# A hybrid encoder's up projections: four chunks by seven products in place of six, begun one tile ahead, with their block sums on VectorE

## The chip, the cores and the metric

The kernel runs on one core of one Trainium2 chip. The metric is the device time of one execution in microseconds (us); of several runs the median is given. A second number per kernel comes from a profiled execution, whose trace has the start and the end of every instruction on TensorE (PE; its weight loads apart as PEld), VectorE (DVE), ScalarE (ACT), GpSimd (POOL) and the DMA queues.

## The reference

Two layers, one sequence of 512 tokens, 1024 features, all in float32. Layer 1 mixes the tokens by gated linear attention, layer 2 by grouped-query softmax attention. Each mixer is followed by the gated feed-forward part (FFN) that this change is about:

```python
D_MODEL, SEQ, DEPTH, D_FF = 1024, 512, 2, 2816

def conv_ffn(h, w_up, w_conv, b_conv, w_down):
    u = h @ w_up                                  # 1024 -> 2 x 2816
    u = lax.conv_general_dilated(u, w_conv[:, None, :], window_strides=(1,),
        padding=[(1, 1)], dimension_numbers=('NWC', 'WIO', 'NWC'),
        feature_group_count=u.shape[-1]) + b_conv # each feature: 3 tokens
    val, gate = jnp.split(u, 2, axis=-1)
    return (jax.nn.silu(gate) * val) @ w_down     # 2816 -> 1024

x = x + mixer(rmsnorm(x, norm_mix[i]))
x = x + conv_ffn(rmsnorm(x, norm_ffn[i]), ...)
```

## The kernel before

**Tiles.** Activations lie with features on the 128 partitions and the 512 tokens in the free dimension: `x` is eight tiles of 128x512 (`KC` = 8). The 2 x 2816 up features are 22 chunks `m` (`FC` = 22). A chunk has two tiles of 128 features, the value tile (t = 0) and the gate tile (t = 1).

**Precision.** A float32 product is made from three products of a rounded type (`F32R`): every operand is split into a high part (a ScalarE copy) and a low part (a VectorE subtraction), and the kernel adds high x high, high x low and low x high. A plain tile is thus 8 blocks of features x 3 = 24 matmuls of 512 columns, and a plain chunk 48. These are the matmuls of lines 359 to 361.

**Seven products.** A pair of tiles times pairs of input blocks is a 2x2 block product. It can be made by seven products of blocks in place of eight, from sums and differences of the blocks. The down projection does this for chunks 0 to 15, in two parts (`down_part`, four strips of weights each, `NQ` = 4), and so do the up projections of the chunks in `SEVEN`: 7 products of 12 matmuls of 256 columns, 84 in all (line 810, in `product`). The accumulators are the `r` banks of PSUM. What a chunk by seven products needs beside a plain one:

- sums of the four weight blocks (`Weights.summed`, lines 158, 159, 166 and 172; the argument `by` says on which engine, GpSimd for up and VectorE for down), then the splits of four pieces. Piece 0 serves the products 1 and 7, piece 1 the products 6 and 5, piece 2 the products 2 and 4, and piece 3 product 3 (`PLACE`). Piece 2 gets its low part by an accumulating DMA that GpSimd issues (`flush`, line 194).
- differences of the input blocks, made once per layer for the four pairs of feature blocks (`prepare_input(p)`, called after chunk p = 0 to 3; tiles `x1`, `x2`, `q`, `xt`). The two subtractions of 256 columns there (lines 889, 890) run on GpSimd, and so do those of `prepare` (lines 866, 867), which does the same for the FFN's middle activations (`gu`) ahead of the down projection.
- sums of products. `seven_up` avoids some by copying a bank into another and letting the next product accumulate on the copy: product 1 is copied into the second bank (line 820), the sum of 1 and 6 into the third (`r3`, the copy below it). Product 3 accumulates on the second bank after its contents were copied to the output tile `d` (line 829). At the end come VectorE's additions and the multiplication by the norm's factor `R`.

After either kind of chunk `act_up` does the convolution: one ScalarE step (line 848) and two VectorE steps of 511 columns (849, 850) per tile, then the activation (852) and the product of the two tiles (853).

**Weights ahead.** `Weights.todo` is the list of all weight pieces in the order in which they are made. A piece is a strip's load into one of two `raw` tiles, perhaps its sums, and its split into `wh` and `wl` (three buffers each, line 204 on ScalarE and 205 on VectorE; `ring`, one buffer, for piece 1 of the sums; `sq`, three buffers, for piece 3). `W.piece(..., ahead)` hands out a piece and makes so many more that `ahead` stand ready; the table `ahead` in `ffn` raises that number near a chunk or part by seven products.

**Order.** The loop at the end of `ffn` runs over m: `act_up(m)`, for m < 4 `prepare_input(m)`, after every second chunk `prepare` or the plain splits, and after m = 9 and m = 17 a part of the down projection (`DOWN_AFTER`). That part is a generator: its product 1 and the copy after it are issued inside `plain_up(m)`, between the chunk's two tiles, and the rest after the chunk. The chunks 16 to 21 go down by plain matmuls at the end, in the order of `PLAIN`. Each engine runs its own instructions in the order in which they are issued here, and waits for others by semaphores. PSUM has three banks `acc` (value tiles, the first two product banks), two `s` (gate tiles, the third bank), two `pt` and one `po`.

## Time and profile before

| | |
|---|---|
| median of three runs | 1145.89 us (1145.68 to 1147.14) |
| profiled execution | 1147.76 us, of which the span from the first to the last instruction is 1146.0 |
| mean granted TensorE clock | 0.990 |
| read from HBM | 100.21 MB |

How to read the rows below. A row of the page names an engine, its busy time in us, the share of the span and the number of instructions. In the stretches (windows), the columns are start:end in us from the span's start, length, then busy us (instructions) of PE, PEld, DVE, ACT and POOL, the mean granted clock (1.00 is full speed), the busy share of the DMA engines, and GB/s. A row of the timeline has start, duration, engine, line, operation, output<-inputs, sizes, and in brackets what the instruction waited for and how long. A row of the waits says which instruction waited for which, total us, times, longest. Lines are those of the kernel before.

### The profile page before, as it was taken

Reading aid. Unit: us, or ns where it says so; the run is one execution under the profiler, and the core shown is the slowest. Engines: PE = TensorE matmul, PEld = TensorE weight load, DVE = VectorE, ACT = ScalarE, POOL = GpSimd, SP = SyncE. Lnnn points to the kernel's source line nnn. Section 1 sums busy time; section 2 is a strip of 40 time slices with the busy share of each in tenths; the row PEclk is TensorE's granted clock in tenths of the full one; section 3 lists DMA queues with packets and bytes.
Section 4 is the critical chain, followed back from the end, with each engine's and each line's share of the span. In section 5 each row is a group of like instructions: output and inputs, shape, how many; then the busy total and the mean of one; then the engine's idle time right before and its main releaser. Section 6 shows DMA issues by size and latency. Waiting matters only on the chain.

```text
span 1146.0 us, 16132 instructions
## 1 busy us (share of the span) xinstructions
PE 1110.6 (97%) x6212; PEld 967.6 (84%) x6212; DVE 863.5 (75%) x1333; ACT 630.2 (55%) x1022; POOL 210.0 (18%) x202
## 2 busy tenths in 40 slices
PE   9999999997999999999999999999799999999998
PEld 7888888885889988899888888788588998889887
DVE  6686774679988778887765588567998877988772
ACT  5565343546656456665464777555664645656550
POOL 0100122014311131122004333001431112112300
PEclk9999999998999999999999999999899999999999
DMA  6323122322416433354447755432241544335442
GB/s 223 132 90 110 56 92 74 111 74 59 129 71 165 134 125 106 103 145 134 144 144 166 193 166 156 129 110 74 58 130 71 159 136 129 95 96 151 139 129 74
DMA packets 33149, 136.91 MB, mean 119 GB/s; under 512 B 4016, under 2 KB 4528, under 8 KB 22704
## 3 DMA queue, kind: packets, MB, share of 16 engines
q1 hardware_dynamic: 21072, 102.16, 25.9%
q0 software_dynamic: 7104, 25.17, 11.2%
q10 hardware_dynamic: 4896, 8.55, 2.0%
q8 instruction: 49, 0.80, 0.3%
q14 instruction: 28, 0.23, 0.1%
HBM read 100.21 MB, written 2.10 MB: 89 GB/s over the span
## 4 chain that ended last, share of the span: by engine, by line
PE 75%; DVE 11%; issue 5%; ACT 4%; POOL 3%; DMA 2%; ACTq 0%; POOLq 0%; DVEq 0%; SPq 0%
PE r L810 17%; PE vg L391 8%; PE op L417 8%; PE up L359 7%; PE up L360 7%; PE up L361 7%; PE dn L360 2%; PE dn L361 2%; PE dn L359 2%; DVE wl L205 1%; DVE y L849 1%; DVE gu L860 1%; DVE y L853 1%; DVE u L798 1%; PE o L685 1%
## 5 line engine op out<-in xcount | busy, mean ns | idle before, releaser
L359 PE MATMUL up<-xhl,wh 128*128 128x512 f32 x512 | 200.7, 392 | 7.3 <-ACT wh L204 7.3
L361 PE MATMUL up<-xhl,wl 128*128 128x512 f32 x512 | 199.5, 390 | 0.6 <-DVE wl L205 0.6
L360 PE MATMUL up<-xhl,wh 128*128 128x512 f32 x512 | 199.9, 391 | 0.0
L204 ACT ACTIVATE wh<-raw 128x1024 fp32r<-128x1024 f32 x108 | 114.0, 1056 | 146.1 <-PE up L360 51.7
L205 DVE TENSOR_TENSOR wl<-raw,wh 128x1024 fp32r<-128x1024 f32 x108 | 131.8, 1220 | 44.2 <-ACT wh L204 43.7
L359 PEld LDWEIGHTS up<-xhl,wh 128*128 128x128 f32 x512 | 96.4, 188 | 27.1 <-ACT wh L204 7.8
L810 PE MATMUL r<-gu,wh 128*128 128x256 f32 x640 | 116.7, 283 | 0.1
L361 PEld LDWEIGHTS up<-xhl,wl 128*128 128x128 f32 x512 | 96.2, 188 | 21.3 <-DVE wl L205 1.4
L360 PEld LDWEIGHTS up<-xhl,wh 128*128 128x128 f32 x512 | 96.5, 188 | 19.0
L810 PEld LDWEIGHTS r<-gu,wh 128*128 128x128 f32 x640 | 99.6, 191 | 0.8 <-ACT r L934 0.5
L194 POOL DMA_DIRECT2D wl<-raw x44 | 39.2, 890 | 287.1 <-ACT wl L145 76.3
L810 PE MATMUL r<-gu,wl 128*128 128x256 f32 x320 | 90.5, 283 | 1.0 <-DMA wl<-raw 1.0
L848 ACT ACTIVATE y<-u,cw 128x512 f32<-128x512 f32 x88 | 69.9, 810 | 35.9 <-DVE u L798 25.4
L391 PE MATMUL vg<-wh,xhl 128*128 128x512 f32 x256 | 80.9, 395 | 1.0 <-DVE wh L202 1.0
L417 PE MATMUL op<-oT,wh 128*128 128x512 f32 x256 | 71.8, 394 | 0.6 <-ACT p L1137 0.6
L849 DVE SCALAR_TENSOR_TENSOR y<-u,cw,y 128x511 f32<-128x511 f32 x88 | 66.3, 766 | 6.7 <-ACT y L848 6.7
L850 DVE SCALAR_TENSOR_TENSOR y<-u,cw,y 128x511 f32<-128x511 f32 x88 | 67.2, 780 | 1.2
L810 PEld LDWEIGHTS r<-gu,wl 128*128 128x128 f32 x320 | 61.1, 191 | 1.2 <-DMA wl<-raw 1.2
L810 PE MATMUL r<-xhl,wh 128*128 128x256 f32 x288 | 56.5, 294 | 4.1 <-ACT u L829 3.7
L391 PEld LDWEIGHTS vg<-wh,xhl 128*128 128x128 f32 x256 | 48.9, 191 | 11.5 <-ACT sq L333 1.3
L798 DVE TENSOR_TENSOR u<-up,R 128x512 f32<-128x512 f32 x64 | 43.5, 683 | 17.5 <-PE up L361 17.5
L859 ACT ACTIVATE gu<-y 128x512 fp32r<-128x512 f32 (+1 forms) x60 | 33.9, 572 | 41.2 <-POOL y L867 19.3
(266 smaller groups left out, 2591.4 us busy)
## 6 DMA issues: line engine op xcount, KB each, us to landing
raw<-in_w_up_dram SPq DMA_DIRECT2D x42, 1024.0 KB, 4.9
wl<-raw POOLq DMA_DIRECT2D x44, 512.0 KB, 4.6
raw<-in_w_down_dram SPq DMA_DIRECT2D x22, 1024.0 KB, 4.9
raw<-in_w_vg_dram SPq DMA_DIRECT2D x6, 1024.0 KB, 4.9
ring<-p ACTq DMA_DIRECT2D x22, 256.0 KB, 3.4
raw<-in_w_kq_dram SPq DMA_DIRECT2D x4, 1024.0 KB, 4.8
raw<-in_w_gout_dram SPq DMA_DIRECT2D x4, 1024.0 KB, 5.0
raw<-in_w_aout_dram SPq DMA_DIRECT2D x16, 256.0 KB, 4.8
```

Source lines behind the costliest of these rows:

```text
L204: act.activation(hi[:, sl], r[:, sl], AF.Copy)
L205: dve.tensor_tensor(lo[:, sl], r[:, sl], hi[:, sl].bitcast(F32), ALU.subtract)
L359: mm(ps, wh, mh, start=start, stop=False)
L360: mm(ps, wh, ml, start=False, stop=False)
L361: return mm(ps, wl, mh, start=False, stop=stop)
L391: mm(ps[j][:, :width], hl[k][i == 2][:, j * P : (j + 1) * P], (wl if i == 1 else wh)[:, sl], start=k == 0 and i == 0, stop=k == KC - 1 and ...
L417: mm(pss[ng][n], wt[:, sl], mv, start=k == 0 and i == 0, stop=k == KC - 1 and i == 2)
L798: dve.tensor_tensor(u, ps, norm.R, ALU.mult)
L810: mm(dst, w[:, sl], m, start=start and j == 0 and a == 0, stop=j == len(pairs) - 1 and a == 2, skip_group_check=True)
L848: act.activation(y, u, AF.Identity, scale=w(1), bias=w(3))
L849: dve.scalar_tensor_tensor(y[:, 1:], u[:, : S - 1], w(0), y[:, 1:], ALU.mult, ALU.add)
L850: dve.scalar_tensor_tensor(y[:, : S - 1], u[:, 1:], w(2), y[:, : S - 1], ALU.mult, ALU.add)
```

## The change

The chunks by seven products become 5, 12, 19 and 21 in place of 4, 6, 12, 14, 18 and 20. They are begun as the parts of the down projection are: `seven_up` is now a generator that `plain_up` of the chunk before starts after its first tile, and that stops after product 1 and the copy into the second bank. `add_up` moves the first piece of its weights ahead of the second half of the chunk before, and the table `ahead` gets the same three entries as for a down part. Products 7 and 6 change places. Product 3 gets a bank `r5` of its own; its output half is then a copy of that bank and an addition from the second bank, and the fourth bank is copied to both halves of `d`, to which the second and third banks are added. That makes five copies of 256 columns on ScalarE per chunk where there were four. All block sums and differences that GpSimd did go to VectorE.

```diff
-SEVEN = (4, 6, 12, 14, 18, 20)
+SEVEN = (5, 12, 19, 21)
...
-        def summed(self, raw, h, by):
+        def summed(self, raw, h):
             a21, a11, a12, a22 = (raw[:, n * S : (n + 1) * S] for n in range(4))
             if h == 0:
                 r = tmp("t", "sum")
                 with tc.issue_after(self.last.ins) if self.last else ExitStack():
-                    by.tensor_tensor(r, a21, a11, ALU.add)
-                    by.tensor_tensor(a21, a21, a22, ALU.add)
+                    dve.tensor_tensor(r, a21, a11, ALU.add)
+                    dve.tensor_tensor(a21, a21, a22, ALU.add)
...
             if h == 1:
-                by.tensor_tensor(a11, a21, a11, ALU.add)
+                dve.tensor_tensor(a11, a21, a11, ALU.add)
...
-                by.tensor_tensor(r, a11, a12, ALU.add)
+                dve.tensor_tensor(r, a11, a12, ALU.add)
...
     def add_up(layer, chunks):
         for m in chunks:
-            W.add(up[layer], (m,), 4 if m in SEVEN else 2, pool)
+            W.add(up[layer], (m,), 4 if m in SEVEN else 2)
+            if m in SEVEN:
+                W.todo[-5:-3] = W.todo[-4], W.todo[-5]
...
         ahead = {(m + i // 2, i % 2): n for m in DOWN_AFTER for i, n in ((-1, 2), (0, 2), (1, 5))}
-        ahead.update({(m - 1, t): 2 for m in SEVEN for t in range(2)})
+        ahead.update({(m - 1 + i // 2, i % 2): n for m in SEVEN for i, n in ((-1, 2), (0, 2), (1, 5))})
...
                 feature_tile(*W.half(up[layer], 2 * m + t, ahead.get((m, t), 1)), norm.hl, ps)
                 pss.append(ps)
+                if t == 0 and m + 1 in SEVEN:
+                    begun.append(seven_up(m + 1))
+                    next(begun[-1])
...
-            r1, r2 = (bank("acc", n)[:, :H] for n in ("r1", "r2"))
+            r1 = bank("acc", "r1")[:, :H]
             go(1, r1, True)
+            r2 = bank("acc", "r2")[:, :H]
             act.activation(r2, r1, AF.Copy)
-            r4 = bank("pt", "r4")[:, :H]
-            go(7, r4, True)
+            yield
             go(6, r2, False)
             r3 = bank("s", "r3")[:, :H]
             act.activation(r3, r2, AF.Copy)
+            r4 = bank("pt", "r4")[:, :H]
+            go(7, r4, True)
             go(2, r1, False)
+            c, d = tmp("u", "u"), tmp("u", "u")
+            dve.tensor_tensor(c[:, :H], r1, norm.R[:, :H], ALU.mult)
             go(5, r2, False)
-            c, d = tmp("u", "u"), tmp("u", "u")
-            act.activation(d[:, H:], r2, AF.Copy)
-            dve.tensor_tensor(c[:, :H], r1, norm.R[:, :H], ALU.mult)
             go(4, r3, False)
-            dve.tensor_tensor(d[:, H:], d[:, H:], r4, ALU.add)
-            go(3, r2, False)
-            act.activation(d[:, :H], r3, AF.Copy)
-            dve.tensor_tensor(d[:, :H], d[:, :H], r4, ALU.add)
-            dve.tensor_tensor(c[:, H:], r2, norm.R[:, H:], ALU.mult)
+            r5 = bank("pt", "r5")[:, :H]
+            go(3, r5, True)
+            act.activation(d[:, :H], r4, AF.Copy)
+            act.activation(d[:, H:], r4, AF.Copy)
+            dve.tensor_tensor(d[:, H:], d[:, H:], r2, ALU.add)
+            dve.tensor_tensor(d[:, :H], d[:, :H], r3, ALU.add)
+            act.activation(c[:, H:], r5, AF.Copy)
+            dve.tensor_tensor(c[:, H:], c[:, H:], r2, ALU.add)
+            dve.tensor_tensor(c[:, H:], c[:, H:], norm.R[:, H:], ALU.mult)
             yield c
...
-            for t, u in enumerate((seven_up if m in SEVEN else plain_up)(m)):
+            for t, u in enumerate(begun.pop() if m in SEVEN else plain_up(m)):
...
-            pool.tensor_tensor(q[:, :H], b22, b12, ALU.subtract)
-            pool.tensor_tensor(b12, b11, b12, ALU.subtract)
+            dve.tensor_tensor(q[:, :H], b22, b12, ALU.subtract)
+            dve.tensor_tensor(b12, b11, b12, ALU.subtract)
```

The last four lines stand for `prepare` and `prepare_input` alike.

What this does to the order of the instructions is seen at two places. The first is ScalarE's queue around chunk 12 of the first layer, which is by seven products before and after. `r` are the product banks, `y` the convolution's tiles, `raw` a strip of weights, `wh` the high part of its split; `wh_3734` and `wh_3752` before, `wh_3609` and `wh_3613` after are the two halves of the plain chunk 13's weights. Before:

```order
L848 ACTIVATE y_3665<-u_3663,cw 128x512
L204 ACTIVATE wh_3734<-raw_3732 128x1024
L848 ACTIVATE y_3671<-u_3669,cw 128x512
L820 ACTIVATE r_3694<-r_3693 128x256
L204 ACTIVATE wh_3752<-raw_3732 128x1024
L852 ACTIVATE y_3671<-y_3671 128x512
L825 ACTIVATE r_3750<-r_3694 128x256
```

After:

```order
L827 ACTIVATE r_3598<-r_3576 128x256
L859 ACTIVATE y_3643<-u_3641,cw 128x512
L204 ACTIVATE wh_3609<-raw_3607 128x1024
L859 ACTIVATE y_3649<-u_3647,cw 128x512
L831 ACTIVATE r_3683<-r_3598 128x256
L204 ACTIVATE wh_3613<-raw_3607 128x1024
L863 ACTIVATE y_3649<-y_3649 128x512
```

The copy into the second bank (L820, now L827) stood behind a weight split and two convolution steps and now stands ahead of them. The copy into the third bank (L825, now L831) stood behind both splits of chunk 13 and now stands between them.

The second place is VectorE's queue in the second layer, where the `ring` tile of the layer's first chunk by seven products (m = 4 before, m = 5 after) gets its low part on line 188. `xt` are the split input differences, `gu` those of the middle activations, `q` differences, `sum` a sum of weight blocks. Before:

```order
L205 TENSOR_TENSOR wl_7585<-raw_7522,wh_7584 128x1024
L849 SCALAR_TENSOR_TENSOR y_7560<-u_7558,cw,y_7560 128x511
L163 TENSOR_TENSOR wl_7594<-raw_7588,wh_7593 128x512
L850 SCALAR_TENSOR_TENSOR y_7560<-u_7558,cw,y_7560 128x511
L893 SCALAR_TENSOR_TENSOR q_7568<-x_7566,x_7567 128x256
L163 TENSOR_TENSOR wl_7594<-sum_7590,wh_7593 128x512
L853 TENSOR_TENSOR y_7554<-y_7554,y_7560 128x512
L860 TENSOR_TENSOR xt_7573<-x_7566,xt_7573 128x256
L860 TENSOR_TENSOR xt_7574<-q_7568,xt_7574 128x512
L895 SCALAR_TENSOR_TENSOR x_7567<-q_7568,x_7567 128x256
L188 TENSOR_TENSOR ring_7625<-raw_7588,ring_7625 128x1024
L860 TENSOR_TENSOR xt_7573<-x_7567,xt_7573 128x256
```

After:

```order
L871 TENSOR_TENSOR xt_7565<-x_7558,xt_7565 128x256
L906 SCALAR_TENSOR_TENSOR x_7559<-q_7560,x_7559 128x256
L871 TENSOR_TENSOR xt_7566<-q_7560,xt_7566 128x512
L878 TENSOR_TENSOR y_7444<-y_7444 128x256
L871 TENSOR_TENSOR xt_7565<-x_7559,xt_7565 128x256
L871 TENSOR_TENSOR gu_7579<-y_7546,gu_7579 128x512
L871 TENSOR_TENSOR gu_7578<-y_7444,gu_7578 128x512
L885 SCALAR_TENSOR_TENSOR q_7575<-y_7444,y_7546 128x256
L188 TENSOR_TENSOR ring_7622<-raw_7509,ring_7622 128x1024
L887 SCALAR_TENSOR_TENSOR y_7546<-q_7575,y_7546 128x256
```

Before, the `ring` tile's low part came among the last inputs of pair 3, ahead of the split of `x_7567`. Now it comes after all inputs, and after two of the splits of the middle activations (`gu`) of the chunks 2 and 3, with the subtraction of line 878, which was GpSimd's, in the same queue.

More of the change, by code (lines that the diff above doesn't have):

```diff
@@ L120, in __init__, with add @@
             self.todo, self.made, self.raw, self.by_dma, self.pending = [], {}, {}, [], []
-            self.sums, self.last, self.fine = {}, None, []
-        def add(self, src, strips=None, pieces=2, by=None):
+            self.sums, self.last, self.fine = set(), None, []
+        def add(self, src, strips=None, pieces=2):
             for i in strips or range(src.shape[0]):
@@ L126, in add @@
                 if pieces > 2:
-                    self.sums[id(src), i] = by
+                    self.sums.add((id(src), i))
         def make(self, key):
@@ L138, in make @@
             if (id(src), i) in self.sums:
-                self.made[id(src), i, h] = self.summed(self.raw[id(src), i], h, self.sums[id(src), i])
+                self.made[id(src), i, h] = self.summed(self.raw[id(src), i], h)
                 return
@@ L234, in add_ffn @@
             add_up(layer, range(first, m + 1))
-            W.add(down_w[layer], range(part * NQ, (part + 1) * NQ), 4, dve)
+            W.add(down_w[layer], range(part * NQ, (part + 1) * NQ), 4)
             at = len(W.todo) - 4 * NQ - 1
@@ L780, in ffn @@
         inputs = []
+        begun = []
         def plain_up(m):
@@ L888, in prepare_input @@
             b11, b12, b21, b22 = y1[:, :H], y1[:, H:], y2[:, :H], y2[:, H:]
-            pool.tensor_tensor(q[:, :H], b22, b12, ALU.subtract)
-            pool.tensor_tensor(b12, b11, b12, ALU.subtract)
+            dve.tensor_tensor(q[:, :H], b22, b12, ALU.subtract)
+            dve.tensor_tensor(b12, b11, b12, ALU.subtract)
             t = [big(F32R, "xt") for _ in range(2)]
```

## Prediction

> **What bounds the kernel now.** I read the page first, then busy time by stretch of the two feed-forward (FFN) layers, with the stretches cut at the first matmul of each chunk in TensorE's timeline, then TensorE's waits, and last the rows of the engines that it waits for. The page's first part says that TensorE (PE) is the bound:
>
> ```profile
> PE 1110.6 (97%) x6212; PEld 967.6 (84%) x6212; DVE 863.5 (75%) x1333; ACT 630.2 (55%) x1022; POOL 210.0 (18%) x202
> ```
>
> So a gain has to be TensorE work that goes, or a wait of TensorE that goes. The stretches tell what a chunk costs there (columns: length in us, busy us and instructions of PE, PEld, DVE, ACT, POOL, then the granted clock, DMA share, GB/s). First layer:
>
> ```profile
> 273.11:318.79 45.68, 35.76 (x218) 31.71 (x216) 42.04 (x58) 28.54 (x46) 16.72 (x15) 0.89 0.39 116
> 391.61:413.39 21.78, 21.78 (x98) 18.03 (x97) 14.47 (x18) 8.85 (x13) 6.38 (x5) 1.00 0.23 78
> 413.39:425.53 12.14, 10.28 (x86) 10.06 (x84) 8.58 (x12) 6.42 (x11) 3.92 (x4) 1.00 0.63 206
> 436.44:447.83 11.39, 10.54 (x85) 10.13 (x84) 9.75 (x15) 6.89 (x13) 1.82 (x2) 1.00 0.72 220
> 475.06:520.96 45.90, 45.85 (x361) 44.67 (x360) 38.75 (x61) 29.05 (x44) 9.83 (x9) 1.00 0.62 168
> 520.96:530.99 10.03, 10.03 (x87) 10.03 (x85) 4.74 (x8) 4.68 (x8) 2.26 (x2) 1.00 0.63 220
> 541.89:552.22 10.33, 10.29 (x85) 10.08 (x84) 7.63 (x11) 5.94 (x10) 0.89 (x1) 1.00 0.69 210
> ```
>
> 391.61 to 413.39 is two plain chunks (m = 10, 11): 10.89 us each, no wait. 520.96 to 530.99 is a chunk by seven products (m = 18) without a wait: 84 matmuls of 256 columns in 10.03 us, 0.119 us each. Seven products are worth only 0.86 us a chunk, so a wait of one microsecond eats the gain. And they wait: m = 12 takes 12.14 us, m = 14 11.39, m = 20 10.33. The first row holds the chunks 4, 5 and 6; without the plain chunk 5 it is 45.68 - 10.89 = 34.79 us for two, 14.73 more than 2 x 10.03. The second layer is alike:
>
> ```profile
> 817.62:864.40 46.78, 36.75 (x217) 32.42 (x216) 42.98 (x61) 29.53 (x47) 16.67 (x15) 0.85 0.38 113
> 959.01:971.11 12.10, 10.26 (x85) 10.06 (x84) 8.56 (x12) 6.52 (x11) 3.92 (x4) 1.00 0.66 207
> 982.02:993.42 11.40, 10.55 (x85) 10.14 (x84) 9.76 (x15) 6.91 (x13) 1.82 (x2) 1.00 0.77 229
> 1067.78:1077.81 10.03, 10.03 (x87) 10.03 (x86) 4.91 (x8) 4.44 (x9) 2.58 (x2) 1.00 0.70 228
> 1088.71:1098.73 10.02, 10.02 (x85) 10.01 (x84) 7.09 (x11) 5.71 (x9) 0.39 (x1) 1.00 0.77 231
> ```
>
> The twelve chunks cost 34.79 + 12.14 + 11.39 + 10.03 + 10.33 = 78.68 and 35.89 + 12.10 + 11.40 + 10.03 + 10.02 = 79.44, together 158.1 us: more than twelve plain ones (130.7). TensorE's waits in the second layer (total us, times, longest) say for whom:
>
> ```profile
> PE r L810 <- ACT r L820: 4.2, 3, 1.8
> PE up L359 <- ACT wh L204: 3.6, 1, 3.6
> PE r L810 <- ACT u L829: 1.8, 1, 1.8
> PE r L810 <- DVE xt L860: 1.8, 1, 1.8
> PE r L810 <- DMA wl<-raw: 1.0, 1, 1.0
> ```
>
> L820 copies product 1 into the second bank, behind which only product 7 (12 matmuls, 1.43 us) runs before the copy is needed. L829 copies the bank away before product 3 overwrites it. L204 and L860 are weights and inputs of the layer's first such chunk, which begins before they are made. The last is an accumulating DMA, issued by GpSimd behind its sums; after the change GpSimd's queue holds only such DMAs in the FFN, and as this wait came once in sixteen strips I count nothing for it.
>
> **The change, part by part.** *Fewer such chunks.* Eight remain and four become plain. Without any wait this is 8 x 10.03 + 4 x 10.89 = 123.8 us against 158.1, a saving of 34.3 less the waits R that the new form still has.
>
> *Begun one tile ahead.* Product 1 now stands ahead of the second tile of the plain chunk before, so its copy has 5.44 us (a tile) of cover, not 1.43, and the L820 waits go. The down projection already begins so: its 336 matmuls and one plain tile fill 475.06 to 520.96, and (45.90 - 5.44) / 4 = 10.11 us per 84 matmuls leaves no wait.
>
> *Third product in its own bank.* Product 3 waits for no copy, so the L829 waits go. ScalarE makes five copies of 256 columns per chunk in place of four, 0.36 us beside matmuls: nothing.
>
> *Product 7 after product 6.* This holds the first weight tile longer, and there is the new wait. How a ScalarE queue stalls TensorE is seen in chunk 6 before, first on ScalarE, then on TensorE:
>
> ```profile
> 309.99 0.81 ACT L848 ACTIVATE y<-u,cw 128x512 f32<-128x512 f32 x1 [1.49 <-DVE u L798]
> 310.71 0.36 ACT L820 ACTIVATE r<-r 128x256 f32<-128x256 f32 x1
> 311.01 1.04 ACT L204 ACTIVATE wh<-raw 128x1024 fp32r<-128x1024 f32 x1
> ```
>
> ```profile
> 311.13 1.71 PE L810 MATMUL r<-xt,ring 128*128 128x256 f32 x12 [1.84 <-ACT r L820]
> ```
>
> The copy sat behind an instruction that waited. In the new order the copy into the third bank sits behind the weight split of the next chunk, and that split waits until product 7 has freed its buffer. From then ScalarE does the split (1.04), in chunks 12 and 21 a convolution step (0.72 to the next start), and the copy (0.36): 2.12 us. The cover is product 2, 1.43 us; product 5, which overwrites the copied bank, comes next. That leaves 0.7, and 0.2 for the hand-overs (the copy ends at 311.07, TensorE starts at 311.13; a matmul of 256 columns runs 0.28 us for a 0.12 us slot): 0.9 us in chunks 12 and 21, 0.2 in chunk 19, where the convolution step is not in between. In chunk 5 it is more: two copies of inputs stand there in the first layer, 0.57 each by
>
> ```profile
> L859 ACT ACTIVATE gu<-y 128x512 fp32r<-128x512 f32 (+1 forms) x60 | 33.9, 572 | 41.2 <-POOL y L867 19.3 <-DVE y L853 11.5 <-DVE y L876 10.3
> ```
>
> so 1.04 + 1.14 + 0.36 - 1.43 + 0.2 = 1.3. In the second layer two splits, one such copy and one of half the size (0.36) give 2 x 1.04 + 0.57 + 0.36 + 0.36 - 1.43 + 0.2 = 2.1. First layer 1.3 + 0.9 + 0.2 + 0.9 = 3.3, second 2.1 + 2.0 = 4.1. The bounds: nothing, if the split is early as in the down projection, and 2.1 each, what chunk 12 loses now.
>
> *The sums on VectorE.* It takes 16 sums of 512 columns (4 chunks x 4) and 24 subtractions of 256 (12 pairs x 2) per layer from GpSimd. One would fear for an engine that was busy 42.04 of 45.68 us in the first stretch. But look at what GpSimd did to it there, GpSimd first:
>
> ```profile
> 272.15 1.28 POOL L159 TENSOR_TENSOR raw<-raw 128x512 f32<-128x512 f32 x1
> 274.95 1.62 POOL L172 TENSOR_TENSOR sum<-raw 128x512 f32<-128x512 f32 x1
> ```
>
> ```profile
> 272.22 1.50 DVE L893 SCALAR_TENSOR_TENSOR q<-x,x 128x256 f32<-128x256 f32 x1 [1.87 <-POOL x L890]
> 273.64 1.78 DVE L163 TENSOR_TENSOR wl<-sum,wh 128x512 fp32r<-128x512 f32 x1
> 275.35 1.77 DVE L853 TENSOR_TENSOR y<-y,y 128x512 f32<-128x512 f32 x1
> ```
>
> and at the same operations without a GpSimd sum beside them:
>
> ```profile
> 248.24 0.68 DVE L853 TENSOR_TENSOR y<-y,y 128x512 f32<-128x512 f32 x1
> 248.84 0.42 DVE L860 TENSOR_TENSOR xt<-x,xt 128x256 fp32r<-128x256 f32 x1
> 249.18 0.69 DVE L860 TENSOR_TENSOR xt<-q,xt 128x512 fp32r<-128x512 f32 x1
> ...
> 251.11 0.74 DVE L850 SCALAR_TENSOR_TENSOR y<-u,cw,y 128x511 f32<-128x511 f32 x1
> 251.77 1.22 DVE L205 TENSOR_TENSOR wl<-raw,wh 128x1024 fp32r<-128x1024 f32 x1
> 252.91 0.68 DVE L798 TENSOR_TENSOR u<-up,R 128x512 f32<-128x512 f32 x1
> ```
>
> Each VectorE operation was stretched by 1.1 us and ended 0.3 to 0.6 us after the GpSimd sum did. A sum on VectorE itself costs 0.60 to the next start (256 columns 0.34, 511 0.67, 1024 1.14), less than the 1.1 that it cost from GpSimd, so VectorE is no worse off: nothing. The Trainium skill (SBUF — State Buffer, "SBUF: two separate sides") has this as an exclusive lock on a shared port pair: the one that starts first holds it for the whole instruction. The trace agrees (1.77 for 0.68 us on line 853), and the sum stays as it is.
>
> Its order still has to be met in chunk 5. From the layer's first scaling of the up tiles to the low half of the tile for product 6, VectorE has in the second layer 26 operations of 512 columns, 16 of 511, 32 of 256 and 6 of 1024: 15.6 + 10.7 + 10.9 + 6.8 = 44.0 us. They start, and TensorE's chunk 1 starts, at
>
> ```profile
> 786.29 1.28 DVE L798 TENSOR_TENSOR u<-up,R 128x512 f32<-128x512 f32 x2
> ```
>
> ```profile
> 784.27 0.48 PE L359 MATMUL up<-xhl,wh 128*128 128x512 f32 x1
> ```
>
> VectorE is done at 830.3. TensorE needs it after eight tiles, product 1 and two matmuls: 784.27 + 8 x 5.44 + 1.43 + 0.24 = 829.5. That is 0.8 late; I take 1.0. In the first layer three operations of 256 and two of 512 fewer stand before it, 2.2 us, and it is in time. So R = 3.3 + 4.1 + 1.0 = 8.4 us.
>
> *The last chunk.* Number 21 by seven products makes its output later: after the last product come a copy, an add and a multiply (0.36 + 0.34 + 0.34), the convolution of both halves (0.72 + 4 x 0.67), an activation, the product of the halves (0.6 each) and a split (0.6 + 0.6), about 7.2 us in a chain. Ahead of the down tiles that need it stand 48 matmuls on earlier chunks, 10.9 us. It is covered, with 3.7 us for what VectorE still has queued; if that is more, TensorE waits for the rest.
>
> *Clock.* The two longest waits came with a lower granted clock (0.89 and 0.85 in the first rows); that is inside their 14.7 and 15.8 us. A short wait can do it too: chunk 6 lost it in the second layer, not in the first, with the same 1.8 us wait:
>
> ```profile
> 306.25:318.79 12.54, 10.57 (x86) 10.16 (x84) 10.90 (x17) 8.05 (x14) 1.84 (x3) 1.00 0.72 211
> 850.77:864.40 13.63, 11.80 (x85) 11.59 (x84) 11.83 (x20) 9.03 (x15) 1.82 (x3) 0.87 0.65 194
> ```
>
> So each short wait that is left has a small chance of 1.1 us more; it goes into the range. The Trainium skill (TensorE: Matmul & The Clock Gate, "Part 1: The HAM clock gate") would halve the clock only after an idle window of about 3.4 us, which would make that price nothing; the second row speaks against it, after a wait of 1.8 us.
>
> **Sum.** 34.3 - 8.4 = 25.9 us less. The profiled execution took 1147.76 us (span 1146.0), 1.9 above the median of the runs, and no term is tied to that difference, so I take it from the median: 1145.89 - 25.9 = 1120 us.
>
> **Rivals.**
> *No wait is left* (R = 0): for it, the down projection has none with the same beginning; against it, the order of the copies above. 1145.89 - 34.3 = 1111.6. Chance 0.12.
> *Each of the eight keeps a wait like chunk 12's now* (2.1 us, R = 16.9), since the ScalarE queue stays in front of a copy: 1128.5, and 1131 with chunk 5's late low half and one lost clock. For it, every chunk but those after the down projection waits today; against it, the cover. Chance 0.18.
> *Slower: VectorE becomes the bound.* If the stretched operations were not GpSimd's doing, each seven-product chunk puts on VectorE 4 sums (2.4), its splits (2.9), eight small steps of the product (2.3), convolution and product (3.3) and half a pair's inputs (2.1), 13.0 us against TensorE's 10.0. The first chunks then keep their 14.7 + 15.8 and the other six lose 3.0 each: R = 48.5, 1160 us. It decides from R = 34.3 on. The stretched rows speak against it. Chance 0.05.
> *No change*, with R between 32.0 and 36.6, a mixture of the two: chance 0.03.
>
> **The numbers.** My forecast, 1115 to 1126, has 0.62. The range takes in the first rival's and the second's ends, 1111 to 1131. A measurement of this kernel can tell 0.2% from no change (2.3 us): faster 0.62 + 0.12 + 0.18 = 0.92, same 0.03, slower 0.05.
>
> **What would show it.** Right: stretches of 10.0 to 12 us for the chunks 12, 19 and 21, no TensorE wait for the copy of product 1 or before product 3, VectorE operations of 512 columns near 0.68 us throughout the FFN layers, and the remaining waits at the copy into the third bank (L831 of the changed kernel). Wrong: a wait of over 3 us in chunk 5, TensorE waiting for VectorE's weight splits in plain chunks, or waits at the first down tiles for the last chunk's output, which now comes from seven products and passes more steps.

## The result

The changed kernel takes 1110.63 us (median of 4 runs, 1110.01 to 1111.65), the kernel before 1145.79 in the same comparison: a ratio of 0.9692, 95% interval 0.9675 to 0.9709, or 35.2 us less. That is 0.4 us below the low end of the forecast range (1111.0). The first part of the page after:

```profile
PE 1099.6 (99%) x6068; PEld 956.3 (86%) x6068; DVE 852.9 (77%) x1401; ACT 614.8 (55%) x998; POOL 94.5 (9%) x102
```

TensorE's share went from 97% to 99%. The two FFN layers, each from the first up matmul to the end of the last down matmul, before and then after (stretches; columns as before):

```profile
227.62:595.77 368.15, 355.17 (x2102) 315.76 (x2100) 299.57 (x439) 210.00 (x315) 70.61 (x65) 0.99 0.39 117
772.08:1142.44 370.36, 356.30 (x2101) 316.25 (x2099) 291.93 (x426) 198.80 (x297) 69.72 (x63) 0.98 0.37 112
```

```profile
225.46:576.54 351.08, 350.91 (x2030) 310.99 (x2029) 294.43 (x473) 202.15 (x303) 13.33 (x15) 1.00 0.39 119
752.90:1104.74 351.84, 351.32 (x2029) 310.84 (x2027) 286.51 (x460) 191.21 (x285) 11.44 (x13) 1.00 0.37 114
```

The gain lies here: 738.51 - 702.92 = 35.6 us. (The profiled executions differ by 37.75; the 2.2 more passed before the first FFN, where the profiled execution of before started its first matmuls later.) VectorE has 34 instructions more per layer, and yet its busy time is lower, 591.5 to 580.9 us in both layers together, while GpSimd's 70 us per layer are down to 13 and 11. (Four chunks less by seven products relieve VectorE too; e8 below measures what GpSimd's part is.) The chunks by seven products are free of waits: the 72 matmuls behind product 1 in the chunks 5, 12 and 21 of the first layer (19 is the same) and 5 of the second:

```profile
282.75:291.35 8.60, 8.60 (x73) 8.60 (x72) 8.58 (x16) 5.46 (x9) 0.00 (x0) 1.00 0.50 156
398.31:406.91 8.60, 8.60 (x73) 8.60 (x72) 7.86 (x13) 6.34 (x11) 0.00 (x0) 1.00 0.60 207
...
535.26:543.87 8.61, 8.61 (x74) 8.61 (x73) 8.54 (x14) 6.18 (x11) 0.00 (x0) 1.00 0.65 182
...
810.19:819.12 8.93, 8.85 (x74) 8.64 (x72) 8.91 (x15) 5.56 (x9) 0.00 (x0) 1.00 0.46 155
```

8.61 and 1.43 for product 1 make 10.04 us per chunk. Only the second layer's chunk 5 loses anything, 0.3. Of TensorE's waits in the first FFN, where the kernel before had seven rows, one is left, in the down projection (the second layer has the same one, 0.4 us):

```profile
PE r L816 <- ACT r L945: 0.2, 1, 0.2
```

### The profile page after: what moved, and what is told of

Its sections match the earlier page's. It is cut to its first block, busy times and chain, and to the rows that moved or that the text cites. A ratio compares the mean times of both kernels' runs of the same rounds, so it can differ in the third digit from the quotient of the medians.

```text
span 1108.3 us, 15700 instructions
## 1 busy us (share of the span) xinstructions
PE 1099.6 (99%) x6068; PEld 956.3 (86%) x6068; DVE 852.9 (77%) x1401; ACT 614.8 (55%) x998; POOL 94.5 (9%) x102
## 4 chain that ended last, share of the span: by engine, by line
PE 93%; DVE 4%; ACT 1%; DMA 1%; issue 0%; POOL 0%; ACTq 0%; SPq 0%; DVEq 0%
PE r L816 21%; PE up L361 11%; PE up L362 11%; PE up L363 11%; PE vg L393 8%; PE op L419 8%; PE dn L362 2%; PE dn L363 2%; PE dn L361 2%; PE o L687 1%; PE A L361 1%; PE av L393 1%; PE A L363 1%; PE A L362 1%; PE pt L1184 1%; PE q L361 1%
## 5 line engine op out<-in xcount | busy, mean ns | idle before, releaser
L361 PE MATMUL up<-xhl,wh 128*128 128x512 f32 x576 | 224.8, 390 | 0.0
L362 PE MATMUL up<-xhl,wh 128*128 128x512 f32 x576 | 224.4, 390 | 0.0
L363 PE MATMUL up<-xhl,wl 128*128 128x512 f32 x576 | 224.2, 389 | 0.0
L204 ACT ACTIVATE wh<-raw 128x1024 fp32r<-128x1024 f32 x116 | 122.6, 1057 | 142.2 <-PE up L362 58.4
L205 DVE TENSOR_TENSOR wl<-raw,wh 128x1024 fp32r<-128x1024 f32 x116 | 141.5, 1220 | 31.7 <-ACT wh L204 31.4
L363 PEld LDWEIGHTS up<-xhl,wl 128*128 128x128 f32 x576 | 108.1, 188 | 22.6
L361 PEld LDWEIGHTS up<-xhl,wh 128*128 128x128 f32 x576 | 108.2, 188 | 21.8
L362 PEld LDWEIGHTS up<-xhl,wh 128*128 128x128 f32 x576 | 108.2, 188 | 21.6
L860 DVE SCALAR_TENSOR_TENSOR y<-u,cw,y 128x511 f32<-128x511 f32 x88 | 64.4, 746 | 9.9 <-ACT y L859 9.8
L804 DVE TENSOR_TENSOR u<-up,R 128x512 f32<-128x512 f32 x72 | 48.6, 685 | 26.1 <-PE up L363 25.8
L861 DVE SCALAR_TENSOR_TENSOR y<-u,cw,y 128x511 f32<-128x511 f32 x88 | 64.2, 746 | 0.7
L863 ACT ACTIVATE y<-y 128x512 f32<-128x512 f32 x44 | 27.7, 629 | 53.9 <-DVE y L861 53.9
L419 PEld LDWEIGHTS op<-oT,wh 128*128 128x128 f32 x256 | 47.3, 188 | 11.1 <-ACT p L1148 0.9
```

What stands on the lines that cost most here:

```text
L204: act.activation(hi[:, sl], r[:, sl], AF.Copy)
L205: dve.tensor_tensor(lo[:, sl], r[:, sl], hi[:, sl].bitcast(F32), ALU.subtract)
L361: mm(ps, wh, mh, start=start, stop=False)
L362: mm(ps, wh, ml, start=False, stop=False)
L363: return mm(ps, wl, mh, start=False, stop=stop)
L419: mm(pss[ng][n], wt[:, sl], mv, start=k == 0 and i == 0, stop=k == KC - 1 and i == 2)
```

## The experiments

All ratios are to runs of the kernel before made beside them (their medians 1146.0 to 1146.8).

| kernel | median us | ratio, 95% interval |
|---|---|---|
| e1: before, four chunks at the new places | 1138.07 | 0.9924 (0.9911 to 0.9937) |
| e2: changed, all sums back on GpSimd | 1138.48 | 0.9927 (0.9913 to 0.9942) |
| e3: changed, begun at their turn | 1121.47 | 0.9784 (0.9769 to 0.9798) |
| e4: changed, product 3 on the second bank | 1112.70 | 0.9709 (0.9696 to 0.9721) |
| e10: before, all sums on VectorE | 1121.29 | 0.9778 (0.9760 to 0.9797) |
| e8: changed, unused sums on GpSimd besides | 1157.68 | 1.0101 (1.0083 to 1.0118) |
| e9: changed, weights' sums on GpSimd | 1118.46 | 0.9756 (0.9740 to 0.9772) |
| e11: changed, inputs' subtractions on GpSimd | 1125.23 | 0.9810 (0.9796 to 0.9823) |
| e6: changed, no chunk by seven products | 1114.12 | 0.9724 (0.9707 to 0.9740) |
| e13: before, no chunk by seven products | 1119.65 | 0.9764 (0.9751 to 0.9778) |
| e5: changed, six chunks begun ahead | 1115.84 | 0.9730 (0.9717 to 0.9743) |
| e12: changed, seven chunks begun ahead | 1132.46 | 0.9877 (0.9862 to 0.9892) |
| e14: changed, only chunk 5 ahead | 1108.96 | 0.9681 (0.9667 to 0.9694) |
| e17: four late chunks, none ahead | 1110.28 | 0.9680 (0.9667 to 0.9694) |
| e15: five chunks, only chunk 5 ahead | 1108.25 | 0.9666 (0.9653 to 0.9679) |
| e16: six chunks, only chunk 5 ahead | 1113.29 | 0.9711 (0.9698 to 0.9725) |
| e18: the changed kernel again | 1110.18 | 0.9683 (0.9666 to 0.9700) |
| e19: e15 again, on e18's chip | 1106.40 | 0.9653 (0.9636 to 0.9671) |

**Which part of the change earns the time.** Three theories went in: A, beginning a chunk ahead; B, taking the sums off GpSimd; C, fewer chunks at better places.

*e1.* The kernel before with one line changed.

```diff
-SEVEN = (4, 6, 12, 14, 18, 20)
+SEVEN = (5, 12, 19, 21)
```

> The kernel before with SEVEN = (5, 12, 19, 21) and nothing else changed: begun at their turn, sums and differences on GpSimd, product 3 on the second bank. Theory A (the waits come from beginning a chunk only at its turn, with 1.43 us of cover for the copy of product 1 and weights not yet split): the waits stay, about 10 us in chunk 5 of each layer (the two first chunks lost 14.7 and 15.8 together), 2.1 in chunk 12, 1.3 in chunk 19, 0.2 in chunk 21, so some 27 us over the changed kernel's 1110.6: 1137, 1128 to 1143. Theory B (they come from GpSimd's sums, which stretch VectorE): the same, 1128 to 1143. Theory C (too many chunks, and in bad places; the form matters little): 1111 to 1116.

1138.07. C falls: fewer chunks at the new places bring 8 of the 35 us. What is left is nearly all chunk 5 of the two layers, 22.91 and 22.31 us long in place of 10.04, at a granted clock of 0.7:

```profile
281.96:304.87 22.91, 14.45 (x85) 13.64 (x84) 19.32 (x24) 12.54 (x20) 8.24 (x7) 0.70 0.37 111
825.99:848.30 22.31, 13.99 (x86) 13.12 (x85) 19.03 (x23) 11.99 (x19) 8.18 (x7) 0.69 0.32 101
```

*e2.* The changed kernel with the sums of the up weights, and all four subtractions of `prepare` and `prepare_input`, on GpSimd; the down weights' sums stay on VectorE, as before the change.

```diff
-                self.made[id(src), i, h] = self.summed(self.raw[id(src), i], h)
+                by = pool if any(src is a for a in up) else dve
+                self.made[id(src), i, h] = self.summed(self.raw[id(src), i], h, by)
...
-            dve.tensor_tensor(q[:, :H], b22, b12, ALU.subtract)
-            dve.tensor_tensor(b12, b11, b12, ALU.subtract)
+            pool.tensor_tensor(q[:, :H], b22, b12, ALU.subtract)
+            pool.tensor_tensor(b12, b11, b12, ALU.subtract)
```

> The changed kernel with the block sums of the up weights and the subtractions of both inputs back on GpSimd. Theory A (begun ahead pays): the copies and weights have a tile of cover, so little comes back, 1111 to 1115, and what does shows in chunk 5, where VectorE is fullest. Theory B (GpSimd's sums on the way of VectorE cost the time): stretched operations of 1.8 us return, 40 GpSimd operations per layer of 1.1 us each, and a good part of it reaches TensorE: 1120 to 1135. Theory C: 1111 to 1113.

1138.48: A falls, since 27.9 us come back, and B, which had 1135 at most, has too little. With sums on GpSimd, beginning ahead, the new product order and the new bank together bring nothing that can be told (e1 0.9924, e2 0.9927). Chunk 4's second tile, ahead of which product 1 now stands, takes 11.43 us for 5.45 of work:

```profile
279.78:291.21 11.43, 8.17 (x24) 5.95 (x25) 10.32 (x17) 7.28 (x13) 4.35 (x5) 0.70 0.25 94
```

TensorE waits for the tile's own weights: 2.1 us for the high half just before this stretch and 2.5 us for the low half in it. Most of the rest is the lower clock. The waits between 255 and 300 us show why the weights are late:

```profile
ACT xt L871 <- POOL x L902: 5.8, 3, 2.6
...
PE up L364 <- DVE wl L206: 2.8, 2, 2.5
...
PE up L362 <- ACT wh L205: 2.1, 1, 2.1
```

(L871 and L902 are one line further than in the changed kernel.) ScalarE, which has to split those weights, stands three times before the split of an input that waits for GpSimd's subtraction; one of these waits, 2.57 us, comes ahead of the split of the weights. And VectorE, which makes the low half, is stretched again: GpSimd's sum first, then VectorE, then the same operation (line 871 there) in the changed kernel:

```profile
271.80 1.61 POOL L160 TENSOR_TENSOR raw<-raw 128x512 f32<-128x512 f32 x1
```

```profile
272.19 1.77 DVE L872 TENSOR_TENSOR xt<-q,xt 128x512 fp32r<-128x512 f32 x1
```

```profile
269.85 0.68 DVE L871 TENSOR_TENSOR xt<-q,xt 128x512 fp32r<-128x512 f32 x1
```

*e10.* The other direction: the kernel before, with nothing but the engine changed. Six chunks at the old places, begun at their turn, product 3 on the second bank.

```diff
-            W.add(up[layer], (m,), 4 if m in SEVEN else 2, pool)
+            W.add(up[layer], (m,), 4 if m in SEVEN else 2, dve)
...
-            pool.tensor_tensor(q[:, :H], b22, b12, ALU.subtract)
-            pool.tensor_tensor(b12, b11, b12, ALU.subtract)
+            dve.tensor_tensor(q[:, :H], b22, b12, ALU.subtract)
+            dve.tensor_tensor(b12, b11, b12, ALU.subtract)
```

> The kernel before with its sums and differences on VectorE, and nothing else changed: chunks 4, 6, 12, 14, 18, 20, begun at their turn. If GpSimd's part was the cause of most waits: the two first chunks lose 3 to 7 in place of 15 per layer, and 12 and 14 lose 1 in place of 3.4: 1118 to 1128. If the places and the number of chunks are the cause: 1138 to 1146.

1121.29: the engine alone brings 25 of the 35 us. Chunks 6, 12 and 14 of the first layer, which took 12.54, 12.14 and 11.39 us:

```profile
299.68:309.70 10.02, 10.02 (x86) 10.02 (x85) 8.96 (x15) 6.97 (x11) 0.00 (x0) 1.00 0.72 218
404.30:414.32 10.02, 10.02 (x85) 10.01 (x84) 9.18 (x16) 7.25 (x13) 0.00 (x0) 1.00 0.80 238
425.23:435.25 10.02, 10.02 (x86) 10.02 (x84) 9.91 (x17) 7.57 (x13) 0.00 (x0) 1.00 0.75 232
```

The waits for the copies of lines 820 and 829 are gone in these chunks, with the lines of the copies as they were. They had stood behind other waits of ScalarE. In chunk 12 the copy of line 829 stood behind a split that waited 3.05 us for GpSimd's subtraction (line 867, behind a sum in GpSimd's queue), and TensorE waited 1.86 us for the copy. ScalarE before, then the same split in e10:

```profile
423.04 0.63 ACT L859 ACTIVATE gu<-y 128x512 fp32r<-128x512 f32 x1 [3.05 <-POOL y L867]
423.58 0.36 ACT L829 ACTIVATE u<-r 128x256 f32<-128x256 f32 x1
```

```profile
411.19 0.63 ACT L859 ACTIVATE gu<-y 128x512 fp32r<-128x512 f32 x1 [0.29 <-DVE y L867]
```

In the chunks 6 and 14 the copy of line 820 stood behind a convolution step that waited 1.49 us for VectorE (line 848 for line 798, for chunk 6 in the rows ahead of the forecast). VectorE was late in chunk 6 after GpSimd as well: ScalarE's split of the `ring` tile waited 2.01 us for GpSimd's sum (line 166), and VectorE's half of that split, stretched from 1.22 to 1.65 us, came behind it. But in these two chunks the order of ScalarE's queue moved with the edit: in e10 the copy stands ahead of that step. So the 25 us are those of the engine together with the order of the queues that came with it; no run holds the order fixed. What stays is in the first stretch, chunks 4 and 5, at 29.46 us, where one wait for the copy of line 820 (1.9 us) is left:

```profile
270.22:299.68 29.46, 24.85 (x134) 21.70 (x132) 27.80 (x49) 18.67 (x30) 1.53 (x2) 0.88 0.34 99
```

*e3.* The changed kernel without the generator.

```diff
-            if m in SEVEN:
-                W.todo[-5:-3] = W.todo[-4], W.todo[-5]
...
-        ahead.update({(m - 1 + i // 2, i % 2): n for m in SEVEN for i, n in ((-1, 2), (0, 2), (1, 5))})
+        ahead.update({(m - 1, t): 2 for m in SEVEN for t in range(2)})
...
-                if t == 0 and m + 1 in SEVEN:
-                    begun.append(seven_up(m + 1))
-                    next(begun[-1])
...
-            yield
+            r4 = bank("pt", "r4")[:, :H]
+            go(7, r4, True)
             go(6, r2, False)
...
```

> The changed kernel, but a chunk begins at its turn: no generator, no moved weight piece, the old entries of the ahead table, products in the order 1, 7, 6, 2, 5, 4, 3. Sums stay on VectorE and product 3 in its own bank. Theory A: the copy of product 1 waits again in ScalarE's queue, 0.7 to 2 us in each of eight chunks, and the first chunk of each layer waits 4 to 8 us for weights: 1122 to 1138. Theory B: VectorE has no stretched operations, so only 2 to 4 us come back: 1112 to 1116. Theory C: 1111 to 1114.

1121.47, just under A's range (from 1122) and above B's (to 1116): with the sums on VectorE, beginning ahead, with its product order and its `ahead` table, is worth 10.8 us. But not where A has it. Chunk 5 of each layer lost 4.8 and 5.0, chunk 12 (between them) nothing, and neither did 19 and 21:

```profile
281.44:296.33 14.89, 11.32 (x85) 10.29 (x84) 14.17 (x24) 10.07 (x16) 0.95 (x1) 1.00 0.45 120
401.82:411.84 10.02, 10.02 (x85) 10.01 (x84) 9.21 (x16) 7.61 (x13) 0.00 (x0) 1.00 0.79 254
813.66:828.73 15.07, 11.32 (x85) 10.30 (x84) 14.36 (x24) 9.74 (x16) 0.91 (x1) 1.00 0.46 120
```

*e4.* The changed kernel with the end of a chunk as before, four copies.

```diff
-            r5 = bank("pt", "r5")[:, :H]
-            go(3, r5, True)
-            act.activation(d[:, :H], r4, AF.Copy)
-            act.activation(d[:, H:], r4, AF.Copy)
+            act.activation(d[:, H:], r2, AF.Copy)
             go(4, r3, False)
+            go(3, r2, False)
```

> The changed kernel with the old end of a chunk: product 3 accumulates on the second bank after ScalarE copied it to the output tile, four copies in place of five, the additions as before the change. If the wait for that copy is a matter of ScalarE's queue behind a weight split, it is 1.8 us in the chunks 12 as in the kernel before, and 0.5 to 1.8 in the others: 1115 to 1124. If beginning ahead has moved the splits out of its way as well, product 4 (1.43 us) covers the copy and nothing comes back: 1110 to 1112.

1112.70. The median is 2.1 us above the changed kernel's, the intervals overlap, and the trace has no TensorE wait in the chunks. So no run shows that the bank is worth anything.

**What GpSimd does to the others.** Theory B1: it stretches VectorE. B2: its results come late, and others wait for them.

*e8.* The changed kernel with sums on GpSimd that nobody reads, of the sizes and at the places of e2's; one scratch tile, for which GpSimd's DMA ring gave up 2 KB.

```diff
+                for _ in range((2, 1, 0, 1)[h]):
+                    pool.tensor_tensor(unused, a12, a22, ALU.add)
...
+            for _ in range(2):
+                pool.tensor_tensor(unused[:, :H], b22, b22, ALU.add)
```

> The changed kernel, its sums and differences on VectorE, and besides as many sums of the same sizes on GpSimd as the sums-on-GpSimd kernel had, whose results nobody reads (16 of 512 columns and 24 of 256 per layer, from the same weight strips and input tiles; GpSimd's DMA ring is 2 KB smaller to make room for their output). Theory B1 (GpSimd's use of the memory stretches VectorE's operations, and that is the 28 us): 1125 to 1138, with operations of 512 columns at 1.8 us near the spare sums. Theory B2 (the sums are slow on GpSimd and wait in its queue, and other engines wait for them): nothing reads these, so 1110 to 1114.

1157.68, 47 us more than the changed kernel and slower than the kernel before. B2 alone falls, since no engine computes with these sums. The stretch shows directly: VectorE's instructions in the two FFN layers are as many as in the changed kernel, and they take 619.8 us in place of 580.9. And the harm runs in both directions. GpSimd in chunk 4, then VectorE, in rows of the same time:

```profile
280.56 13.06 POOL L908 TENSOR_TENSOR unused<-x 128x256 f32<-128x256 f32 x2 [7.89 <-ACT x L905]
293.56 0.95 POOL L199 DMA_DIRECT2D wl<-raw  x1
294.23 1.64 POOL L883 TENSOR_TENSOR unused<-y 128x256 f32<-128x256 f32 x2
```

```profile
280.55 1.40 DVE L866 SCALAR_TENSOR_TENSOR y<-u,cw,y 128x511 f32<-128x511 f32 x2
281.87 0.41 DVE L909 TENSOR_TENSOR q<-x,x 128x256 f32<-128x256 f32 x1
...
291.18 1.21 DVE L210 TENSOR_TENSOR wl<-raw,wh 128x1024 fp32r<-128x1024 f32 x1
292.51 0.64 DVE L876 TENSOR_TENSOR gu<-y,gu 128x256 fp32r<-128x256 f32 x1
293.07 1.63 DVE L210 TENSOR_TENSOR wl<-raw,wh 128x1024 fp32r<-128x1024 f32 x1
```

Two operations that take 1.64 us together elsewhere take 13.06, and 12.31 of that is the first one's. They start with a VectorE instruction under way, and VectorE then runs without a gap until 292.39. GpSimd's first operation ends 0.5 us after that, its second at 293.62. The accumulating DMA stands behind them in GpSimd's queue, and TensorE waits for it:

```profile
298.19 0.58 PE L821 MATMUL r<-xhl,wl 128*128 128x256 f32 x1 [6.60 <-DMA wl<-raw]
```

The Trainium skill (SBUF — State Buffer, "SBUF: two separate sides") has whichever of the two engines starts first keep the SBUF port pair that they share for its whole instruction. This trace agrees with the exclusion, and here GpSimd did not get in between the instructions of a VectorE without a gap. That is no rule: in e2's rows above, GpSimd's sum did get in, and VectorE, which had no gap from 269.5 to 275.2 either, was stretched. What decides between the two is open. So e8 holds two costs at once, the stretch and the late DMA, and its 47 us can't be put down to the first alone.

*e9 and e11.* e2's two halves: only the weights' sums, then only the subtractions (the first and the second part of e2's diff).

> The changed kernel with the block sums of the up weights on GpSimd, and the subtractions of the inputs on VectorE. With both on GpSimd it was 1138.5. Theory B1 (stretch, by GpSimd's time): the weights' sums are about half of it, 1122 to 1128. Theory B2 (waiting for the sums): the weights of chunk 5 are what TensorE waits for, 1131 to 1139.

> The changed kernel with only the subtractions of both kinds of inputs back on GpSimd (24 of 256 columns per layer); the weights' sums stay on VectorE. Both together cost 27.9 us, the weights' sums alone 7.8. Theory D1 (the two add): 20 come back, 1129 to 1133. Theory D2 (the subtractions hurt because they stand behind the weights' sums in GpSimd's queue, and the queues of ScalarE and VectorE behind them): alone they cost little, 1112 to 1118.

1118.46 and 1125.23: 7.8 and 14.6 of the 27.9 us; the remaining 5.5 appear only when both are there. Neither D1 (20 us) nor D2 (7 at most) had the subtractions right, and B1 and B2 both had too much for the weights' sums: the smaller operations cost more. With the subtractions alone, GpSimd's and ScalarE's rows in chunk 4, then TensorE at product 6 of chunk 5:

```profile
278.75 1.44 POOL L900 TENSOR_TENSOR q<-x,x 128x256 f32<-128x256 f32 x1 [9.60 <-ACT x L898]
280.27 1.06 POOL L901 TENSOR_TENSOR x<-x 128x256 f32<-128x256 f32 x1
```

```profile
281.36 0.42 ACT L870 ACTIVATE xt<-x 128x256 fp32r<-128x256 f32 x1 [2.69 <-POOL x L901]
...
287.74 0.36 ACT L827 ACTIVATE r<-r 128x256 f32<-128x256 f32 x1
```

```profile
288.15 1.22 PE L816 MATMUL r<-xt,ring 128*128 128x256 f32 x4 [4.45 <-ACT r L827]
```

The copy of product 1, begun a tile ahead and still waited for, stands behind ScalarE's wait of 2.69 us for GpSimd. This is a wait for a late result, as B2 has it, like the one in chunk 12 of the kernel before. So both theories hold a part: e8 shows a stretch without any late result, and these rows show late results on the way to TensorE. How the 25 to 28 us divide between the two was not measured.

*e6 and e13.* SEVEN empty in the changed kernel, and in the kernel before; the input differences are made and not used.

```diff
+SEVEN = ()
```

> The changed kernel with SEVEN empty: all 22 up chunks plain (the input differences are still made, and not used). If the eight chunks are now free of waits, they are worth 8 x 0.86 us: 1117.5, 1116 to 1119. That would also say that the kernel before lost by its twelve chunks, some 28 us. If VectorE's extra work for such chunks still costs elsewhere, less: 1111 to 1115.

> The kernel before with SEVEN empty: no up chunk by seven products, the input subtractions still on GpSimd (the input differences are made and not used). The changed kernel without such chunks took 1114.1. Theory D2 (GpSimd's part hurts only where a chunk by seven products waits for it): 1113 to 1117. If its stretching of VectorE costs everywhere in the FFN: 1120 or more.

1114.12 and 1119.65. So the kernel before lost 27 us by its twelve chunks against no such chunk at all, and the changed kernel's eight gain 3.5 (at 0.86 each it would be 6.9, and the FFN stretches of the two traces differ by 4.8; where the rest goes was not located). The 5.5 between e6 and e13 are what GpSimd's subtractions cost where no up chunk is by seven products: in e13 TensorE waits 2.4 us per layer for VectorE's low half of a plain chunk's weights (L361 <- DVE wl L205), in e6 not at all. They are smaller than the 14.6 of e11, and 1119.65 lies between the two expectations (1117 at most, 1120 or more).

**How much of it should be begun ahead.** *e5 and e12*: the changed kernel with SEVEN = (5, 7, 12, 14, 19, 21), and with 16 besides.

> The changed kernel with six chunks per layer, SEVEN = (5, 7, 12, 14, 19, 21). The eight are worth 3.5 us over plain ones, 0.43 each. If the two more per layer are as free of waits, 1.7 to 3.4 less: 1107 to 1109. If VectorE has no room for them between the others (each needs about 13 us of VectorE in 10.0 us of TensorE, a plain chunk about 9.6 in 10.9): waits of 1 to 3 each, 1111 to 1118.

> The changed kernel with seven chunks per layer, SEVEN = (5, 7, 12, 14, 16, 19, 21). Free of waits: 2.6 to 5.2 less than the changed kernel, 1105.5 to 1108. If VectorE has no room: 1112 to 1122, with TensorE waiting for VectorE's low halves.

1115.84 and 1132.46, both slower than four chunks, the second by more than was expected (1122 at most); e12's waits are of e5's kinds, and for the accumulating DMA besides (2.9 and 4.1 us per layer). In e5's first layer, chunk 14 waits for the low half of its tile for product 6; the plain chunk 9, the second after chunk 7, waits for the low half of its weights, and the down part behind it for a copy:

```profile
PE r L816 <- DVE ring L188: 1.4, 1, 1.4
PE r L816 <- ACT r L939: 1.4, 1, 1.4
PE up L363 <- DVE wl L205: 1.2, 1, 1.2
PE up L361 <- DVE u L804: 0.7, 1, 0.7
```

Yet in e10 chunk 14, begun at its turn, cost nothing. Hence theory E: only the first chunk of a layer needs to be begun ahead. *e14, e17, e15, e16* have a second list in the changed kernel:

```diff
+AHEAD = (5,)
...
-            for t, u in enumerate(begun.pop() if m in SEVEN else plain_up(m)):
+            for t, u in enumerate(begun.pop() if m in AHEAD else (seven_up if m in SEVEN else plain_up)(m)):
```

Chunks that aren't in it are made as in e3. e14 keeps SEVEN; e17 has (12, 14, 18, 20) and nothing ahead; e15 has (5, 12, 14, 18, 20), e16 7 besides.

> The changed kernel with only chunk 5 begun ahead; 12, 19 and 21 begin at their turn with products in the order 1, 7, 6, 2, 5, 4, 3. Theory E (beginning ahead matters only for the first chunk of a layer, whose weights and inputs come late): 1110 to 1112. If it covers waits in the other chunks too: 1113 to 1120.

> The changed kernel with SEVEN = (12, 14, 18, 20), all begun at their turn: no chunk of the crowded part of the layer, nothing begun ahead. Theory E: as many chunks, no waits, 1109 to 1112. If chunks begun at their turn wait by the form: 1114 to 1122.

> SEVEN = (5, 12, 14, 18, 20), chunk 5 begun ahead and the others at their turn. Theory E: one chunk more per layer without waits, 0.4 to 0.9 us each, so 1109 to 1110. If VectorE has no room for chunk 14 beside 12, as in the kernel with six: 1112 to 1115.

> SEVEN = (5, 7, 12, 14, 18, 20), chunk 5 begun ahead and the others at their turn. Theory E: two chunks more per layer, 1107.5 to 1109. If chunk 7 makes VectorE late for the down projection that follows (3 us per layer in the kernel with six begun ahead): 1112 to 1116.

1108.96, 1110.28, 1108.25, 1113.29. E holds: e14 and e17 are not slower than the changed kernel, and e17 begins nothing ahead and has no chunk before 12. e16 misses E's range (1109 at most) by chunk 7, all that it has more than e15: TensorE waits in each layer 0.9 us for VectorE's low half in the plain chunk 9 and 1.3 us for the copy in the down part, and e15 has neither wait. *e18 and e19* put the changed kernel and e15 on one chip.

> The changed kernel again, beside the next one: 1109.5 to 1111.5.

> The kernel with SEVEN = (5, 12, 14, 18, 20), chunk 5 alone begun ahead, beside the one before: if the chunk more per layer is worth something, 0.8 to 2.4 us less than it; if not, within 0.5.

1110.18 (1109.02 to 1111.00) and 1106.40 (1105.84 to 1108.14): e15's form is 3.8 us faster, more than the 0.8 to 2.4 expected, with no run of one among those of the other. Its first layer:

```profile
225.19:575.13 349.94, 349.90 (x2066) 311.91 (x2064) 299.68 (x483) 206.44 (x312) 14.16 (x16) 1.00 0.40 121
```

The FFN stretches of the two traces give 1.9 of it (702.21 to 700.34); the rest lies outside them and isn't explained.

## Why the prediction was wrong

**The saving of 34.3 was right.** Chunks without a wait take 10.04 us, and 10.03 was forecast. The forecast failed by R and by a gain that it put at nothing.

**R: 8.4 forecast, 0.3 measured. First step: "that split waits until product 7 has freed its buffer".** It did not. ScalarE in chunk 12 of the changed kernel:

```profile
398.27 1.06 ACT L204 ACTIVATE wh<-raw 128x1024 fp32r<-128x1024 f32 x1 [3.89 <-PE up L362]
399.24 0.81 ACT L859 ACTIVATE y<-u,cw 128x512 f32<-128x512 f32 x1
399.95 0.37 ACT L831 ACTIVATE r<-r 128x256 f32<-128x256 f32 x1
401.26 1.06 ACT L204 ACTIVATE wh<-raw 128x1024 fp32r<-128x1024 f32 x1 [0.94 <-PE r L816]
```

The split ahead of the copy took the buffer of the plain tile, whose last use of it ended just before 398.27, ahead of product 6. It is the second split that waited for product 7, and that one stands behind the copy, as the order rows above show. The copy ended at 400.32, and TensorE needs it at 402.62. So 2.3 us were to spare where 0.9 were to be lost. The queue order was read; which of the three buffers a piece gets was not. That is 7.4 of the 8.4: the same step gave the copy's waits of all eight chunks, and none of them is there.

**Second step: the low half for product 6 in the second layer's chunk 5, 1.0.** VectorE was late, and by more:

```profile
810.72 1.22 DVE L188 TENSOR_TENSOR ring<-raw,ring 128x1024 fp32r<-128x1024 f32 x1
```

```profile
810.19 0.41 PE L816 MATMUL r<-xt,ring 128*128 128x256 f32 x2
810.43 0.40 PE L816 MATMUL r<-xt,wh 128*128 128x256 f32 x2
...
811.51 0.40 PE L816 MATMUL r<-xt,wh 128*128 128x256 f32 x2
811.99 1.45 PE L816 MATMUL r<-xt,ring 128*128 128x256 f32 x10
```

It ended at 811.94, 1.5 us after the 810.43 at which product 6 wanted it. But in the order of TensorE's queue, matmuls of product 7, whose weights are ready, stand there ahead of the rest of product 6. Only 0.3 was lost. The VectorE sum was close (830.3 - 784.27 = 46.0 us after chunk 1's start; measured 811.94 - 765.09 = 46.9); TensorE's side was not read from the order.

**What was put at nothing.** The kernel before also lost time in the plain tiles ahead of its first chunk by seven products. Its two stretches from chunk 1 to that chunk hold six tiles, 33.31 and 33.35 us; the same stretch after holds seven tiles and takes 38.19 us in each layer, 5.46 a tile. So 0.6 was lost per layer. Before, then after (first layer):

```profile
239.80:273.11 33.31, 33.05 (x148) 27.05 (x146) 28.71 (x43) 20.56 (x32) 9.53 (x10) 1.00 0.22 76
784.27:817.62 33.35, 33.05 (x147) 27.04 (x145) 28.52 (x43) 21.14 (x33) 9.73 (x10) 1.00 0.22 77
```

```profile
237.65:275.84 38.19, 38.19 (x171) 31.62 (x169) 37.59 (x66) 25.52 (x41) 0.00 (x0) 1.00 0.21 70
```

The single wait for the accumulating DMA, in a down part, went too (1.0). That is 2.2, of which the waits for a copy in the down parts (L945, 0.2 and 0.4) gave 0.6 back: 34.3 - 0.3 + 1.6 is the 35.6 of the stretches. So the step that set the low end, R = 0 with nothing below it, failed too; the plain tiles and the DMA wait had something to gain.

**The causes were the other way round.** The forecast put the sums on VectorE at nothing and gave the vanishing of the waits to the cover of a tile and to the new bank. The runs show the engine as the main part (25 us alone in e10, 27.9 in e2), the bank as worth nothing that can be told (e4), and the cover as worth nothing without the engine and 10 us with it, nearly all in chunk 5. That the 34.3 came out is luck in part: with what the forecast counted on but without the engine (e2), the kernel is no faster than with neither (e1), and the waits would have stayed. The forecast had rows that say where they come from: ScalarE's line 859, which it used for the length of a copy, stood idle 19.3 us for GpSimd's line 867, and a step ahead of the copy in chunk 6 waited 1.49 us for VectorE. It did not ask why the two were late. It used the stretched rows only to show that VectorE is no worse off.

**The rivals.** R = 0 came closest (1111.6). The slower one needed VectorE to be the bound without GpSimd; its condition is refuted by e10, though e5 and e12 show the bound from the other side, with too many chunks. The clock term was right to be kept out of the middle: the granted clock is 1.00 in all stretches after. In e2 it fell around waits of 2.1 and 2.5 us with 0.7 us between them (0.70 in the quoted stretch). The Trainium skill (TensorE: Matmul & The Clock Gate, "Part 1: The HAM clock gate") gives an idle window of about 3.4 us for it; neither wait alone is as long as that.

## What to carry to other kernels

When a row shows an operation at two or three times its usual length, look for what ran beside it on GpSimd. Price moving that work by following the lateness through the queues, not by the engine's own balance: here ScalarE waited for a result of GpSimd (3.05 us in chunk 12 before) or for a late VectorE (1.49 us in chunk 6), and the copy that TensorE waited for stood behind that wait. In this kernel, beginning a chunk ahead helped only in the first chunk of a layer, whose weights and inputs come late. Before costing a wait for a buffer, find in the trace of a like place which release the instruction waited for.

## What was not expected of the hardware

Two GpSimd operations of 256 columns, 1.64 us otherwise, took 13.06 while VectorE ran from instruction to instruction without a gap (e8), and a DMA in GpSimd's queue stood behind them, for which TensorE waited 6.60 us. In e2, GpSimd's sum got in beside a VectorE without a gap, and VectorE's operation took 1.77 us in place of 0.68.
